# Exponential and normalising moved one step later in the chunk-band attention, and the stick-breaking gates loaded once, in a hybrid streaming encoder layer

## The chip, the core and the metric

The kernel runs on one core of one Trainium2 chip. The core has five engines that work side by side, each through its own list of instructions in the order of that list: PE (TensorE, matrix products and transposes), DVE (VectorE), ACT (ScalarE), POOL (GpSimd) and SP (SyncE, which here only issues transfers). The engines wait for each other by semaphores. The metric is the device time of one execution in microseconds (us); lower is better. Before the change it is 1001.7 us, the median of three runs from 1001.65 to 1001.97 us.

## What is computed

The reference is one layer of an encoder trunk over 1024 prompt tokens and 64 tokens of a running stream (whose past has 512 tokens). Everything is float32. Cut to what matters:

```python
h = rms_norm(x, norm_w) @ w_in                       # 1024 -> 6144 columns
sb_q, sb_k, sb_v, sb_z, cb_q, cb_k, cb_v, cb_z, g_sb, g_cb = split(h)
# branch A, "sb": stick-breaking attention, 8 heads x 64, causal over all keys
A[t, s] = beta[t, s] * prod_{s<j<t} (1 - beta[t, j]),   beta = sigmoid(q.k / 8)
# branch B, "cb": softmax attention over a band of 576 keys, with a bias by relative position
s = q.k / 8 + rel_bias[clip(q_pos - k_pos, -128, 128)]
p = softmax(s)
# merge
b_sb = (o_sb * silu(z_sb)) @ w_proj_sb
b_cb = (o_cb * silu(z_cb)) @ w_proj_cb
y = x + (sigmoid(g_sb) * b_sb + sigmoid(g_cb) * b_cb) @ w_out
```

A softmax of branch B is an exponential of the scores less their maximum, and a multiplication of each row by one over its sum. The keys, the values and `y` are outputs.

## The kernel before, in words

The kernel is written with an order of its own: every engine executes its instructions in the order in which the program emits them, and a tile framework adds the semaphores. A tile pool hands out a fixed number of buffers for each name; whoever takes a buffer again waits until the last reader of its earlier content is done.

**Stages.** The program first projects the input, then runs the attention of both branches, first all of "sb", then all of "cb", each as a list of steps (`seq`). It ends with the projection of "cb" and the output projection. A matrix product at full precision is split into three products of a high and a low part, so PE has much to do throughout.

**Attention steps.** One step is one head (or, for the stream tokens, both heads of a pair) with 128 query rows. Each branch has four pairs of heads, and each pair 17 steps: one for the stream tokens (`t == 8`, 576 keys) and two for each of eight blocks of 128 prompt tokens. In "cb" a block has 128 keys (t = 0) to 640 keys (t from 4 to 7), so 32 of its 68 steps have the full width of 640. The loop at the end of the attention code runs over steps `i`, and step `i` emits work for several of them:

- `qk(i)`: PE makes the scores `z` (two PSUM tiles when there are more than 512 keys, of three in the pool). For "cb" DVE adds the bias, negated, and keeps the row's minimum in `sm` (line 1041, two halves); then, as the last line of `qk`, ACT makes the exponential and its row sum (line 1045).
- `mid(i - 1)`: for "cb" DVE takes the reciprocal of the row sum (line 1058) and ACT multiplies the row by it (line 1059). `be` is the row of scores, exponentials and weights; it has four buffers.
- `tr(i - 3)` (`LAG` is 3): PE transposes the finished rows in blocks of 128 into PSUM tiles `pt` (line 1087; two buffers, up to four blocks in each), and ACT or DVE copies them to `wT` (lines 1096 and 1098). In "cb" every fourth of these copies is ACT's.
- `av`, one step after the second head of a pair of blocks: PE multiplies `wT` with the values into `o` (line 1126), and DVE multiplies that by the branch's gate z (line 1131).
- `fill`: between these parts PE gets matrix products that have nothing to do with the attention, by a count for each step.

**The filling work** comes from one generator, `run_fill`. It does eight units of 128 columns of the input projection (the gate columns of "cb", line 782, with a copy by ACT on line 757), and after these `proj_sb`, the projection of branch A. `proj_sb` is a list of twelve jobs `j`, four pieces of 256 output columns for three groups of tokens (384, 384 and 320, `CH`). Each job has two halves (`uu`): 12 matrix products into one of two PSUM tiles `acc` (line 882), and then a multiplication by the sigmoid of the branch's gate on DVE (line 886). That gate has been stored to DRAM before and comes back through `load_gate` (line 862): two transfers by SP into a tile `gt`, which has two buffers. Before the change a job loads the next job's gate at its start, and once more after the first half:

```python
            load(j + 1)                 # at the start of job j
            ...
                if uu == 0:
                    load(j + 1)         # again, after its first half
```

Where the second load takes the buffer that job j itself reads, SP cannot issue it before the multiplication of job j's second half, and SP's list stands until then.

**The end of the attention.** What remains of `proj_sb` after the last step (jobs 8 to 11 in part) runs by itself, and beside it the outputs of "cb" are read back from DRAM (line 839, `ot`, two buffers of two pairs each) and split into a high part on ACT (line 843) and a low part on POOL and DVE (line 848, `og`), for three groups of tokens. On DVE the two low parts of a group stand between the multiplications of `proj_sb`. The next group's outputs can be loaded only when the group before has been split. Then come the projection of "cb" (line 926) and the output projection (line 1429).

Of the kernel before, what the change touches and what calls it, by code (L numbers as in the profile page):

```python
# [32 lines left out]
def hybrid_step_kernel(ctx: ExitStack, tc: tile.TileContext, x_prompt, x_sample, c_sbk, c_sbv, c_cbk, c_cbv,  # L33
# [830 lines left out]
    def proj_sb(pool):  # L864
        load = lambda j: j < 12 and load_gate(pool, "gt", j, d_g["sb"][2 * (j // 3):2 * (j // 3) + 2], j % 3)
        for j in range(12):
            i, ci = divmod(j, 3)
            wh, wl = W.sp["p", i]
            a, e = CH[ci]
            load(j + 1)  # L870
            if ci == 0:
                load_proj(i + 2)
            if ci == 1:
                W.split(("p", i + 1))
            gt = gts.pop(j)
            for uu in range(2):
                cw = slice(uu * 128, uu * 128 + 128)
                ps = psF.tile([128, 512], F32, name="acc")
                for p in range(NPAIR):
                    gh, gl = og("sb", 0, p), og("sb", 1, p)  # L880
                    for m, (w, g) in enumerate(((wh, gh), (wh, gl), (wl, gh))):
                        TE.matmul(ps[:, :e - a], w[:, p, cw], g[:, a:e], start=p == 0 and m == 0,  # L882
                                  stop=p == NPAIR - 1 and m == 2)
                        if p < NPAIR - 1 or m < 2:
                            yield 1
                V.tensor_tensor(out=tb(2 * i + uu)[:, a:e], in0=ps[:, :e - a], in1=gt[:, uu, :e - a], op=OP.mult)
                if uu == 0:
                    load(j + 1)
                yield 1

    def load_gcb(j):
# [119 lines left out]
    def qk(i):  # L1011
# [17 lines left out]
        for j, (x, y) in enumerate(hs):  # L1029
# [10 lines left out]
            else:  # L1040
                V.tensor_tensor_reduce(be[:r, x:y], z[:r, :m], bt[:r, off + x:off + y], 1.0,  # L1041
                                       BIG if j == 0 else kp[:r, j - 1:j], OP.add, OP.min, kp[:r, j:j + 1])
        if b == "cb":
            j = len(hs) - 1
            A.activation(be[:r, :n], be[:r, :n], AF.Exp, bias=kp[:r, j:j + 1], scale=-1.0, accum_out=kp[:r, 2:3])  # L1045
        st[i] = (be, kp)

    def mid(i):
        b, p, t, hd = seq[i]
# [138 lines left out]
    for i in range(len(seq) + LAG + 1):  # L1188
        m = 0
        if i < len(seq):  # L1190
            b, p, t, hd = seq[i]
            if b == "cb" and p == 0 and t == 8 and hd == 0:
                sbx.close()
                yst = ExitStack()
                late["y"] = yst.enter_context(tc.tile_pool(name="ay", bufs=2))
            if (b, p, t, hd) == ("sb", 3, 6, 0):
                load_bias(0)
                load_bias(1)
            qk(i)
            if hd == 0:  # L1200
                if t % 2 == 1 or t == 8 and (b, p) != ("sb", 0):
                    load_z(b, p, t // 2 if t < 8 else 4)
                prefetch(b, p, t)
            acc += amount[b] * wt[b](band(b, t)[1]) / tot[b]
            if (b, p, t) == ("cb", 0, 8):
                acc += 12
            m = int(acc) - emitted
            emitted += m
        if 0 < i <= len(seq):
            mid(i - 1)  # L1210
        flush()
        if i < len(seq) and seq[i][:3] == ("cb", 0, 1) and hd == 1:
            late["sb"] = True
        fill(m // 2)
        while avq:
            av(*avq.pop(0))
        if 0 <= i - LAG < len(seq):
            tr(i - LAG)
            b, p, t, hd = seq[i - LAG]
            if t == 8 or hd == 1 and t % 2 == 1:  # L1220
                avq.append((b, p, t // 2 if t < 8 else 4))
        fill(m - m // 2)
# [292 lines left out]
```

## Time and profile before

The profiled execution took 1000.43 us, 1.27 us less than the median of the runs; its span is 998.6 us, and 1.8 us lie around the span.

| part | what it is | us |
|---|---|---|
| median of three runs | 1001.65 to 1001.97 | 1001.7 |
| profiled execution, whole | one run | 1000.43 |
| its span | first to last instruction | 998.6 |
| PE, matrix products | 97% of the span | 966.4 |
| DVE | 63% | 631.9 |
| ACT | 51% | 510.0 |
| POOL | 35% | 346.6 |

In the span the "cb" attention begins at about 673 us, its last products with the values end at 840 us, the last matrix product of `proj_sb` starts at 862 us, and the output projection starts at 911 us.

How to read the rows. A row of the timeline gives the start, the length, the engine, the line of the kernel, the operation and its tiles (out <- in, without buffer numbers), the shape and how many instructions are merged in it. The bracket at its end is the time that the engine was idle before it and what ended that wait. PEld is PE's loading of weights, which runs beside its products; SPq is the list of transfers that SP issues. A row of the windows gives, for a stretch of the span, each engine's busy time, then PE's granted clock (1.00 is full speed), the share of time that the 16 DMA engines were busy, and their rate in GB/s.

### The profile page before, as it was taken

The numbers are of one execution on the slowest core, as the hardware profiler recorded it, in microseconds if no ns is written. First come the engines' busy times: TensorE is split into PE (matmuls) and PEld (weight loads), VectorE is DVE, ScalarE is ACT, GpSimd is POOL, SyncE is SP. The second block draws the span as 40 slices with busy tenths as digits, with TensorE's granted clock in tenths as the row PEclk, the third lists the DMA queues.
The fourth block names the chain that finished last, engine by engine and source line by source line (L and its number), as shares of the span: only waits on it lengthen the run. The fifth ranks groups of instructions, "written<-read, shape, count | busy, mean of one in ns | idle before, by whom it ended". The sixth has DMA issues, their size and how long they took to land.

```text
span 998.6 us, 20448 instructions
## 1 busy us (share of the span) xinstructions
PE 966.4 (97%) x7568; PEld 917.9 (92%) x7568; DVE 631.9 (63%) x1188; ACT 510.0 (51%) x1142; POOL 346.6 (35%) x356
## 2 busy tenths in 40 slices
PE   5999999999999999999999999999899999899998
PEld 5999999999999999999988889888787877799998
DVE  5456674895455455432169899895676764589735
ACT  5544443444343433433268778786776774355320
POOL 3276663215445544542220110110201101286641
PEclk9999999999999999999999999999999999999999
DMA  6726577424656333332497567575788873853642
GB/s 229 232 95 219 190 249 257 149 91 149 199 156 189 104 94 110 121 108 73 138 254 203 151 164 197 145 212 162 225 241 244 245 208 97 260 170 99 196 137 89
DMA packets 177412, 171.04 MB, mean 171 GB/s; under 512 B 35040, under 2 KB 163168, under 8 KB 177184
## 3 DMA queue, kind: packets, MB, share of 16 engines
q1 hardware_dynamic: 168592, 161.41, 54.1%
q10 hardware_dynamic: 8720, 8.33, 2.6%
q8 instruction: 60, 0.98, 0.4%
q14 instruction: 40, 0.33, 0.1%
HBM read 110.96 MB, written 58.72 MB: 170 GB/s over the span
## 4 chain that ended last, share of the span: by engine, by line
PE 84%; ACT 5%; DVE 4%; DMA 3%; issue 2%; SPq 1%; POOL 1%; DVEq 0%; ACTq 0%
PE b L634 25%; PE acc L464 19%; PE b L1429 8%; PE o L1126 6%; PE acc L782 6%; PE pt L1087 5%; PE b L926 5%; PE z L1035 5%; PE acc L882 2%; DVE be L1041 1%; ACT be L1059 1%; ACT be L1045 1%; ACT wT L1096 1%; DMA wrawx<-in_w_in_dram 1%; PE pk L349 1%
## 5 line engine op out<-in xcount | busy, mean ns | idle before, releaser
L1087 PE MATMUL pt<-ident,be 128*128 128x128 f32 (+1 forms) x568 | 88.5, 278 | 10.0 <-ACT wT L1096 6.9
L122 POOL TENSOR_TENSOR wlo<-wraw,whi 128x1024 fp32r<-128x1024 f32 x22 | 57.2, 2598 | 107.9 <-ACT whi L115 107.7
L1055 DVE TENSOR_TENSOR_SCAN kp<-kp,imp 128x128 f32<-128x128 f32 (+7 forms) x64 | 88.3, 1379 | 0.6 <-ACT kp L1038 0.6
L1087 PEld LDWEIGHTS pt<-ident,be 128*128 128x128 f32 (+1 forms) x568 | 65.5, 140 | 23.0 <-ACT wT L1096 11.0
L1035 PE MATMUL z<-ks,sq 128*128 128x320 f32 (+5 forms) x384 | 83.5, 325 | 0.0
L464 PE MATMUL acc<-whi,xa 128*128 128x256 f32 x256 | 74.1, 292 | 0.0
L1096 ACT ACTIVATE wT<-pt 128x512 f32<-128x512 f32 (+3 forms) x125 | 58.3, 498 | 29.4 <-PE pt L1087 29.3
L464 PE MATMUL acc<-wlox,xm 128*128 128x256 f32 x256 | 70.7, 278 | 0.0
L464 PE MATMUL acc<-whi,xm 128*128 128x256 f32 x256 | 70.7, 278 | 0.0
L464 PE MATMUL acc<-wlo,xa 128*128 128x256 f32 x256 | 70.6, 278 | 0.0
L464 PE MATMUL acc<-whix,xb 128*128 128x256 f32 x256 | 70.6, 278 | 0.0
L464 PE MATMUL acc<-whix,xm 128*128 128x256 f32 x256 | 70.6, 278 | 0.0
L1126 PE MATMUL o<-wT,vp 128*64 128x256 f32 (+1 forms) x608 | 68.5, 357 | 2.0 <-ACT wT L1096 1.0
L1126 PEld LDWEIGHTS o<-wT,vp 128*64 128x64 f32 x608 | 42.7, 136 | 27.2 <-issue 5.9
L1035 PEld LDWEIGHTS z<-ks,sq 128*128 128x128 f32 x384 | 65.9, 188 | 1.3 <-DVE sm L1041 0.3
L1045 ACT ACTIVATE be<-be,sm 128x640 f32<-128x640 f32 (+5 forms) x68 | 47.4, 697 | 35.4 <-DVE sm L1041 34.8
L782 PE MATMUL acc<-xm,whi 128*128 128x384 f32 (+1 forms) x192 | 65.2, 340 | 0.0
L1056 DVE TENSOR_TENSOR be<-be,kp 128x128 f32<-128x128 f32 (+8 forms) x68 | 57.3, 843 | 9.4 <-ACT sg L757 0.5
L1038 ACT ACTIVATE kp<-z 128x384 f32<-128x384 f32 (+6 forms) x104 | 52.2, 502 | 10.1 <-PE z L1035 4.5
L642 DVE TENSOR_TENSOR u<-b,s 128x256 f32<-128x256 f32 (+1 forms) x48 | 20.8, 439 | 55.8 <-PE b L634 54.1
L1039 ACT ACTIVATE be<-z 128x384 f32<-128x384 f32 (+6 forms) x104 | 52.6, 506 | 0.0
L464 PEld LDWEIGHTS acc<-whi,xa 128*128 128x128 f32 x256 | 47.9, 188 | 0.1
(300 smaller groups left out, 3149.9 us busy)
## 6 DMA issues: line engine op xcount, KB each, us to landing
wraw<-in_w_in_dram SPq DMA_DIRECT2D x32, 512.0 KB, 4.5
wrawx<-in_w_in_dram SPq DMA_DIRECT2D x16, 512.0 KB, 4.3
sq<-d_qsbT SPq DMA_DIRECT2D x32, 192.0 KB, 3.6
sq<-d_qcbT SPq DMA_DIRECT2D x32, 192.0 KB, 4.2
gt<-d_gsb SPq DMA_DIRECT2D x30, 192.0 KB, 3.8
xt<-in_x_prompt_dram SPq DMA_DIRECT2D x8, 512.0 KB, 5.6
d_kcbT<-hl SPq DMA_DIRECT2D x8, 512.0 KB, 4.5
d_qcbT<-hl SPq DMA_DIRECT2D x8, 512.0 KB, 5.2
```

What stands on the lines that cost most here:

```text
L122: (eng or G).tensor_tensor(out=l, in0=raw, in1=h[:].bitcast(F32), op=OP.subtract)
L464: TE.matmul(ps, x, w, start=m == 0, stop=m == len(steps) - 1)
L634: TE.matmul(ps[:, :m], w[:, hl_, k], right[s](x)[:, k, a:b], start=s < 3 and k == 0 and e == 0, stop=k == 3 and e == 2, skip_group_check=s ...
L782: TE.matmul(ps[:, :b - a], w[:, k], xk(x, k)[:, a:b], start=k == 0 and n == 0, stop=k == KT - 1 and n == 2)
L1035: TE.matmul(z[:, :m], s[:, e, q0:q0 + 128], ks[:, h, o + x:o + y], start=e == parts[0][0], stop=e == parts[-1][0])
L1045: A.activation(be[:r, :n], be[:r, :n], AF.Exp, bias=kp[:r, j:j + 1], scale=-1.0, accum_out=kp[:r, 2:3])
L1055: V.tensor_tensor_scan(kp[:r, n - 1::-1], kp[:r, n - 1::-1], im[:, ::-1], 0.0, op0=OP.mult, op1=OP.add)
L1056: V.tensor_tensor(out=be[:r, :n], in0=be[:r, :n], in1=kp[:r, 1:n + 1], op=OP.mult)
L1087: TE.transpose(pt[:kr, x, :r], be[:r, kb * 128:kb * 128 + kr], ident[:r, :r])
L1096: A.activation(w[:, sl:sl + m, q0:q0 + r], pt[:, :m, :r], AF.Copy)
L1126: TE.matmul(o[hd * 64:hd * 64 + 64, c0:c1], vv[:kr, kb, hd * 64:hd * 64 + 64], wT[b, p, j, hd, s // 4][:kr, s % 4, c0:c1] if j < 4 else wT ...
L1429: TE.matmul(ps[:, t], left[s](xs_, k)[:, ts_], wt_[:, k], start=s < 3 and t == k == e == 0, stop=k == 3 and e == 2, skip_group_check=s > 2 ...
```

## The change

The exponential leaves `qk` and becomes `soft`, which step `i` calls for the "cb" step `i - 1`, ahead of its own scores. For "cb" `mid`, the reciprocal and the normalising, moves from step `i + 1` to step `i + 2`, also ahead of the scores. For "sb" `mid` stays where it was. The transposes of a row stay three steps behind its scores. And the second load of each gate in `proj_sb` goes.

```diff
@@ proj_sb
                 V.tensor_tensor(out=tb(2 * i + uu)[:, a:e], in0=ps[:, :e - a], in1=gt[:, uu, :e - a], op=OP.mult)
-                if uu == 0:
-                    load(j + 1)
                 yield 1
@@ qk, and the new soft
-        if b == "cb":
-            j = len(hs) - 1
-            A.activation(be[:r, :n], be[:r, :n], AF.Exp, bias=kp[:r, j:j + 1], scale=-1.0, accum_out=kp[:r, 2:3])
         st[i] = (be, kp)
+
+    def soft(i):
+        n = band(*seq[i][::2])[1]
+        be, kp = st[i]
+        j = 1 if n > 512 else 0
+        A.activation(be[:, :n], be[:, :n], AF.Exp, bias=kp[:, j:j + 1], scale=-1.0, accum_out=kp[:, 2:3])
@@ the loop over the steps
+        if 0 < i <= len(seq) and seq[i - 1][0] == "cb":
+            soft(i - 1)
+        if 1 < i <= len(seq) + 1 and seq[i - 2][0] == "cb":
+            mid(i - 2)
+        if i < len(seq):
             qk(i)
@@ the same loop, further down
-        if 0 < i <= len(seq):
+        if 0 < i <= len(seq) and seq[i - 1][0] == "sb":
             mid(i - 1)
```

Where this puts the instructions can be seen at three places. In the rows below, each `be` number is one step's row of scores, and `sm` with the next number is its small tile; the numbers differ between the two programs. Of four steps in a row, the first to the fourth, the rows are be_10514, be_10553, be_10592 and be_10627 before, and be_10502, be_10541, be_10580 and be_10615 after.

ACT, in the third pair of "cb" among steps of the full width, before: L1045 is the exponential, L1059 the normalising, L115 the split of a weight for `proj_sb`, L1096 a copy of transposed blocks (pt_10579 belongs to an earlier row, pt_10647 to be_10514).

```order
L115 ACTIVATE whi_10547<-wraw_9816 128x1024
L1045 ACTIVATE be_10553,sm_10554<-be_10553,sm_10554 128x640
L1059 ACTIVATE be_10514<-be_10514,sm_10515 128x640
L1096 ACTIVATE wT_10578<-pt_10579 128x4x128
L1045 ACTIVATE be_10592,sm_10593<-be_10592,sm_10593 128x640
L1059 ACTIVATE be_10553<-be_10553,sm_10554 128x640
L1045 ACTIVATE be_10627,sm_10628<-be_10627,sm_10628 128x640
L1059 ACTIVATE be_10592<-be_10592,sm_10593 128x640
L1096 ACTIVATE wT_10578<-pt_10647 128x3x128
```

The same place of ACT after the change, where L1047 is the exponential, L1060 the normalising and L1097 the copy; pt_10629 holds blocks of be_10502.

```order
L115 ACTIVATE whi_10532<-wraw_9813 128x1024
L1047 ACTIVATE be_10502,sm_10503<-be_10502,sm_10503 128x640
L1060 ACTIVATE be_10478<-be_10478,sm_10479 128x640
L1097 ACTIVATE wT_10563<-pt_10564 128x4x128
L1047 ACTIVATE be_10541,sm_10542<-be_10541,sm_10542 128x640
L1060 ACTIVATE be_10502<-be_10502,sm_10503 128x640
L1047 ACTIVATE be_10580,sm_10581<-be_10580,sm_10581 128x640
L1060 ACTIVATE be_10541<-be_10541,sm_10542 128x640
L1097 ACTIVATE wT_10563<-pt_10629 128x3x128
```

ACT's list keeps its kinds of work in the same order, but each exponential and each normalising in it is now that of the step before; the copies stay where they were.

DVE at the same place, before: L1041 is the addition of the bias with the row's minimum (two halves, each followed by a reading of the result), L1058 the reciprocal, L1098 a copy of transposed blocks, L1131 the product of an output with its gate.

```order
L1041 ISA be_10553,sm_10554<-z_10555,bias_9916 128x320
L1041 ISA sm_10554 128x1
L1041 ISA be_10553,sm_10554<-z_10559,bias_9916,sm_10554 128x320
L1041 ISA sm_10554 128x1
L1058 RECIPROCAL sm_10515<-sm_10515 128x1
L1131 TENSOR_TENSOR zt_10403<-o_10568,zt_10403 128x256
L1098 COPY wT_10585<-pt_10586 128x128
L1041 ISA be_10592,sm_10593<-z_10594,bias_9912 128x320
```

And DVE after the change (L1039 the addition of the bias, L1059 the reciprocal, L1132 the product, L1099 the copy).

```order
L1059 RECIPROCAL sm_10479<-sm_10479 128x1
L1039 ISA be_10541,sm_10542<-z_10543,bias_9912 128x320
L1039 ISA sm_10542 128x1
L1039 ISA be_10541,sm_10542<-z_10547,bias_9912,sm_10542 128x320
L1039 ISA sm_10542 128x1
L1132 TENSOR_TENSOR zt_10393<-o_10553,zt_10393 128x256
L1099 COPY wT_10570<-pt_10571 128x128
L1059 RECIPROCAL sm_10503<-sm_10503 128x1
L1039 ISA be_10580,sm_10581<-z_10582,bias_9908 128x320
```

The reciprocal of be_10514 (be_10502 after) has moved from behind its own step's successor to behind the product and the copy that follow, right ahead of the next scores.

SP, after the last step of the attention, before: the loads of the "cb" outputs (`ot`, groups of four), of the gates of `proj_sb` (`gt` from d_gsb6 and d_gsb7, two transfers each, for the jobs 9, 10 and 11) and of a weight.

```order
L862 DMA gt_11331<-d_gsb6_99 128x384
L862 DMA gt_11331<-d_gsb7_100 128x384
L862 DMA gt_11348<-d_gsb6_99 128x384
L862 DMA gt_11348<-d_gsb7_100 128x384
L862 DMA gt_11365<-d_gsb6_99 128x384
L862 DMA gt_11365<-d_gsb7_100 128x384
L826 DMA wraw_11368<-in_w_proj_cb_dram 128x4x128 x2
L862 DMA gt_11385<-d_gsb6_99 128x384
L862 DMA gt_11385<-d_gsb7_100 128x384
L839 DMA ot_11406<-d_ocb0_113 128x384
L839 DMA ot_11406<-d_ocb1_114 128x384
```

The same stretch of SP after the change.

```order
L862 DMA gt_11307<-d_gsb6_99 128x384
L862 DMA gt_11307<-d_gsb7_100 128x384
L862 DMA gt_11338<-d_gsb6_99 128x384
L862 DMA gt_11338<-d_gsb7_100 128x384
L826 DMA wraw_11341<-in_w_proj_cb_dram 128x4x128 x2
L839 DMA ot_11376<-d_ocb0_113 128x384
L839 DMA ot_11376<-d_ocb1_114 128x384
L839 DMA ot_11379<-d_ocb2_115 128x384
L839 DMA ot_11379<-d_ocb3_116 128x384
```

Between job 9's gate and the outputs of the second group, SP now has one load of job 10's gate where it had a second load of job 9's and two of job 10's. In the whole program 22 transfers of gates are gone, two for each of the jobs 1 to 11.

## The prediction

> **What bounds the kernel now.** I read the page's summary first, then the windows of the stretches that the change touches, then the list of waits in them, and last the timeline around the longest waits.
>
> ```profile
> span 998.6 us, 20448 instructions
> PE 966.4 (97%) x7568; PEld 917.9 (92%) x7568; DVE 631.9 (63%) x1188; ACT 510.0 (51%) x1142; POOL 346.6 (35%) x356
> ```
>
> PE is busy for 97% of the span, so a change that takes no work from PE can only win PE's idle time. How much of it lies where the change acts is read by stage:
>
> ```profile
> core 0: us, PE busy (x) PEld busy (x) DVE busy (x) ACT busy (x) POOL busy (x), PEclk, DMA share, GB/s
> 673.00:840.00 167.00, 157.26 (x1190) 133.34 (x1189) 111.10 (x396) 115.98 (x261) 16.98 (x22) 1.00 0.72 202
> 840.00:866.00 26.00, 21.12 (x117) 19.70 (x114) 9.24 (x14) 7.63 (x13) 6.74 (x6) 0.93 0.71 220
> 866.00:912.00 46.00, 46.00 (x285) 46.00 (x284) 41.39 (x54) 26.92 (x48) 32.01 (x26) 1.00 0.53 165
> ```
>
> In the "cb" attention (673 to 840) PE is idle for 167.00 - 157.26 = 9.74 us, while ACT and DVE are busy for only 69% and 67%: no engine is full, so the idle time comes from waiting in turn. In the stretch behind it, where `proj_sb` ends alone, PE is idle for another 4.88 us and its granted clock is below 1. In the 46 us after that PE never stops. The waits, with their total, their number and the longest, are these in the first of the stretches, and in the two together for the last three rows:
>
> ```profile
> PE pt L1087 <- ACT wT L1096: 6.3, 8, 1.7
> PE o L1126 <- ACT wT L1096: 1.0, 2, 0.5
> PE o L1126 <- DVE wT L1098: 0.8, 1, 0.8
> PE pt L1087 <- DVE wT L1098: 0.4, 1, 0.4
> ...
> PE acc L882 <- DVE xm L886: 4.9, 4, 3.5
> ACT be L1045 <- DVE sm L1041: 34.8, 34, 2.6
> DVE xm L886 <- DMA gt<-d_gsb: 8.4, 4, 3.6
> ```
>
> Twelve waits of 8.5 us in all hold PE in the attention, ten of them on a copy by ACT. PE wants a PSUM tile for the next transposes, and the copy out of it stands in ACT's list behind an exponential, which waits 34 times for the scores of the newest step. In the last stretch PE waits 4.9 us for DVE's multiplication by the gate, which waits for the gate's transfer.
>
> **Part 1, the exponential and the normalising.** Nothing is added: the same 68 exponentials, reciprocals and normalising copies, and one table load. What moves is where ACT stands when it has to wait. One of the twelve waits shows it:
>
> ```profile
> 785.51 0.83 ACT L1045 ACTIVATE be<-be,sm 128x640 f32<-128x640 f32 x1 [0.95 <-DVE sm L1041]
> 786.34 0.82 ACT L1059 ACTIVATE be<-be,sm 128x640 f32<-128x640 f32 x1
> 786.74 0.71 PE L1087 MATMUL pt<-ident,be 128*128 128x128 f32 x5
> 787.53 0.83 ACT L1045 ACTIVATE be<-be,sm 128x640 f32<-128x640 f32 x1 [0.37 <-DVE sm L1041]
> ...
> 789.08 0.47 ACT L1096 ACTIVATE wT<-pt 128x384 f32<-128x384 f32 x1
> ...
> 789.60 0.77 PE L1087 MATMUL pt<-ident,be 128*128 128x128 f32 x5 [0.68 <-ACT wT L1096]
> ```
>
> PE's transposes are done at 787.45, but ACT copies them only at 789.08: it waited for DVE until 787.53, then made an exponential and a normalising. With the change the pair ahead of that copy is the one of the step before, which ran here from 785.51 to 787.16, so ACT stands ready when the transposes are done. The copy comes some 1.6 us sooner, and the 0.68 us are won. I did the same for each of the twelve; three keep something.
>
> ```profile
> 680.13 1.14 PE L1087 MATMUL pt<-ident,be 128*128 128x128 f32 x8 [1.28 <-ACT wT L1096]
> ...
> 835.85 0.77 PE L1087 MATMUL pt<-ident,be 128*128 128x128 f32 x5 [0.53 <-ACT wT L1096]
> ```
>
> The wait at 835.85 and the one of 0.4 us on DVE's copy, which follows it, belong to the last steps, where PE has no filling work; they stay, since there ACT needs a reciprocal that DVE makes behind copies of fresh transposes, before the change and after it. The wait at 680.13, at the start of "cb", keeps about half, some 0.6 us, because ACT's table load then falls into the next step. That leaves 8.5 - 0.9 - 0.6 = 7.0 us of waits to win.
>
> What is late next: a row's normalising comes a step later and its transposes do not, so only about half a step lies between them, where it was a step and a half. Where ACT has extra work, that is used up:
>
> ```profile
> 699.98 1.05 ACT L115 ACTIVATE whi<-wraw 128x1024 fp32r<-128x1024 f32 x1
> 701.34 0.82 ACT L1045 ACTIVATE be<-be,sm 128x640 f32<-128x640 f32 x1
> 702.15 0.82 ACT L1059 ACTIVATE be<-be,sm 128x640 f32<-128x640 f32 x1
> ...
> 702.34 0.77 PE L1087 MATMUL pt<-ident,be 128*128 128x128 f32 x5
> ...
> 706.66 0.83 ACT L1045 ACTIVATE be<-be,sm 128x640 f32<-128x640 f32 x1 [1.74 <-DVE sm L1041]
> ...
> 709.25 0.44 PE L1087 MATMUL pt<-ident,be 128*128 128x128 f32 x2 [1.69 <-ACT wT L1096]
> ```
>
> Here a weight's split fills ACT from 699.98. With the change the normalising at 702.15 is that of the very row that PE transposes at 702.34, so PE would wait until 702.97, a new 0.6 us; the 1.69 us at 709.25 go, as ACT's 1.74 us of waiting at 706.66 go. I count four such new waits of 0.55 us, for the splits and the reading of "sb" outputs that share ACT with full steps: 2.2 us. On DVE the reciprocal now stands ahead of the newest scores. It needs an exponential that ACT makes first in the step before; I cost it at nothing, covered by most of that step; the cover fails only where ACT is over a step late, and then each us of that holds up the scores, and PE, a PSUM tile further on, by as much. SP, POOL and PE keep their order in this part, and no transfer moves with it. The sum of part 1 is 7.0 - 2.2 = 4.8 us. The trace of before does not show the short spare time itself; its ends are 7.5 us won (no new wait, and all but the two last old ones gone) and a loss, priced below. I take a value nearer to the upper end, because the row at 787.53 is the common case and the one at 702.15 has a split, a gate copy and an output's high part in one step.
>
> **Part 2, the gates.** 22 transfers go, 14 of 192 KB and 8 of 160 KB, 4.0 MB. In the attention they share a queue that is busy for 72%, and PE waits for no transfer there; that share of them I cost at nothing, hidden under the attention steps, and what it costs if the cover fails is the wait on a gate: DVE waited 8.4 us for gates in four places. The gain is in the end of `proj_sb`:
>
> ```profile
> 843.44 5.02 SPq L862 DMA_DIRECT2D gt<-d_gsb  x6
> ...
> 848.66 0.56 DVE L886 TENSOR_TENSOR xm<-acc,gt 128x384 f32<-128x384 f32 x1 [3.63 <-DMA gt<-d_gsb]
> ...
> 851.31 0.54 DVE L886 TENSOR_TENSOR xm<-acc,gt 128x384 f32<-128x384 f32 x1
> 851.88 0.81 SPq L862 DMA_DIRECT2D gt<-d_gsb  x2
> ...
> 852.79 1.80 SPq L839 DMA_DIRECT2D ot<-d_ocb  x4
> ...
> 857.65 2.21 DVE L848 TENSOR_TENSOR og<-ot,og 128x384 fp32r<-128x384 f32 x2 [2.83 <-ACT og L843]
> 859.78 0.54 DVE L886 TENSOR_TENSOR xm<-acc,gt 128x384 f32<-128x384 f32 x1
> ...
> 856.58 0.31 PE L882 MATMUL acc<-xa,wlo 128*128 128x320 f32 x1
> 860.38 0.41 PE L882 MATMUL acc<-xa,whi 128*128 128x320 f32 x1 [3.49 <-DVE xm L886]
> ```
>
> Read backwards: PE stands at 860.38 for the multiplication of 859.78; that stands on DVE behind the low parts of 857.65; these wait for outputs that SP issued at 852.79, behind the second load of a gate at 851.88, which had to wait for the multiplication of 851.31. The multiplication of 848.66 waits for a gate whose first load was issued at 843.44 and whose second one counts. Without the second loads that gate is there one landing after 843.9, and with
>
> ```profile
> gt<-d_gsb SPq DMA_DIRECT2D x30, 192.0 KB, 3.8
> ```
>
> that is 847.7. The multiplication ends at 848.2, the two low parts of the first group, which stand behind it on DVE as those of the second do at 857.65 and take as long (2.2 us), at 850.4, and then SP, with nothing held ahead, issues the last two of the four outputs; before, those two came at 852.79 + 0.9 = 853.7. So the rest of the chain comes 3.3 us earlier, and PE goes on at 857.1 instead of 860.38. It will have come to that place at about 854.9: before, it was there at 856.58 + 0.31, and some 2 us of that were shorter pauses for the two multiplications ahead. So it still stands for some 2.2 us. The ends for this term are 1.5 us (the outputs land no sooner than half of this gain) and 4.9 us (no pause at all). Then there is the clock behind the pause:
>
> ```profile
> 862.00:863.00 1.00, 1.00 (x6) 1.00 (x5) 0.14 (x1) 0.00 (x0) 0.00 (x0) 0.50 0.90 310
> ...
> 700.00:720.00 20.00, 17.63 (x130) 1.00 0.81 240
> 861.00:866.00 5.00, 5.00 (x23) 0.66 0.83 258
> ```
>
> (The first row has all engines, the other two PE alone.) After the pause of 3.49 us the granted clock fell to 0.50 and was 0.66 on the mean of 5 us: 5 x 0.34 = 1.7 us lost. After the pause of 1.69 us at 709.25 the window kept 1.00. A pause of 2.2 us lies between the two; the shorter one is nearer (0.5 against 1.3 us), so I take the 1.7 us as won, with 0 and 1.7 as ends. The Trainium skill says in "TensorE: Matmul & The Clock Gate", part 1, that the clock halves after at least one idle window of about 3.4 us that runs freely; by that rule a pause of 2.2 us cannot halve it, and both pauses above agree with it.
>
> The stage behind, 866 to 912, could take the gain back, since DVE is 90% busy there; but PE waited for nothing in it, DVE's work starts from the same transfers and moves with it, and I take nothing off. Part 2 is 3.3 + 1.7 = 5.0 us.
>
> **Sum.** 4.8 + 5.0 = 9.8 us. Against the profiled execution that is 1000.43 - 9.8 = 990.6 us; that run was 1.3 us below the median of three, and against the median it is 1001.7 - 9.8 = 991.9 us.
>
> **Rivals.**
> - *Only the gates tell.* For each old wait on ACT's copy a new one on the normalising comes, as at 702.34. For it: ACT works without a break in the rows from 699.98 to 702.97. Against it: 34.8 us of ACT's waiting go. Part 1 is 0: 1001.7 - 5.0 = 996.7 us.
> - *The last pause stays.* The outputs land late for another reason (queue 71% busy), PE stands for 3.49 us again and the clock halves again. For it: in the row of 857.65 DVE waits for ACT, not for a gate. Against it: SP's order in the rows of 851.88 and 852.79. 1001.7 - 4.8 = 996.9 us.
> - *Slower: the normalising becomes the wait of every full step.* PE's transposes come where ACT has just begun the row. The price at 702.34 is 0.6 us; in all 32 full-width steps it is 19.2 us, and the time 1001.7 + 19.2 - 9.8 = 1011.1 us. It decides from 9.8 / 32 = 0.3 us a step. Against it: ACT is 69% busy, so it cannot be late in each step.
> - *No change*: PE's work is the same, and the waits come back elsewhere, on DVE's copies for instance; within 0.2% of 1001.7.
>
> **How the numbers follow.** 0.2%, 2.0 us, is about what a measurement of this kernel can tell from no change. Both parts, 988 to 996 us: 0.60. Only the gates, 996.7: 0.12. The last pause stays, 996.9: 0.08. Below 988: 0.05; the floor is 1001.7 - 9.74 - 4.88 - 1.7 = 985.4. Within 0.2%: 0.06. The slower rival: 0.09. So faster is 0.60 + 0.12 + 0.08 + 0.05 = 0.85. The range goes from the upper ends, 7.5 + 4.9 + 1.7 = 14.1 below (987.6, given as 988), to 999, where part 1 gives about 1 and part 2 its lower 1.5; it holds the first three cases, 0.80.
>
> **What would show it.** Right: in the "cb" attention PE's idle time falls from 9.7 to about 5 us, and ACT's waits for DVE's scores almost vanish; some PE waits name the normalising. SP shows 16 gate loads of 192 KB for 30, the outputs are issued some 3 us sooner after the attention's end, and PE's clock stays at 1.00. Wrong: PE waits at many transposes for ACT's normalising, or DVE's reciprocals wait for the exponential and hold up the scores; or the pause at the last job is still over 3 us.

## The result, and the profile after

The changed kernel takes 986.89 us, the median of four runs from 986.66 to 988.42 us; the kernel before took 1001.84 us in the same comparison. The ratio is 0.984, with a 95% interval from 0.980 to 0.988. The forecast was 991.9 us, with a range from 988 to 999: the direction was right, but the time lies below the range, where the forecast had put a chance of 0.05. The gain of 14.9 us is half as large again as the 9.8 us forecast.

The page's summary of the changed kernel:

```profile
span 985.0 us, 20439 instructions
PE 962.0 (98%) x7568; PEld 917.6 (93%) x7568; DVE 630.1 (64%) x1188; ACT 510.4 (52%) x1142; POOL 346.2 (35%) x356
```

Its profiled execution has a span 13.6 us shorter than the one before. Where they went is read from windows cut at the same points of the program: the copy of the last gate columns ahead of "cb", the start of the last product with the values, the first product of the projection of "cb", the first of the output projection. Before:

```profile
core 0: us, PE busy (x) PEld busy (x) DVE busy (x) ACT busy (x) POOL busy (x), PEclk, DMA share, GB/s
672.97:840.30 167.33, 157.59 (x1193) 133.64 (x1192) 111.13 (x396) 116.01 (x261) 16.98 (x22) 1.00 0.71 202
840.30:862.60 22.30, 17.43 (x100) 16.02 (x99) 8.75 (x13) 5.00 (x9) 6.67 (x5) 0.98 0.70 217
862.60:910.90 48.30, 48.30 (x288) 48.30 (x288) 40.81 (x54) 28.63 (x50) 30.98 (x25) 0.97 0.56 175
```

And after:

```profile
673.75:831.80 158.05, 154.21 (x1193) 133.67 (x1192) 109.34 (x396) 116.82 (x261) 17.00 (x22) 1.00 0.70 195
831.80:849.30 17.50, 16.19 (x101) 15.75 (x100) 7.58 (x13) 4.99 (x9) 7.08 (x5) 1.00 0.68 207
849.30:896.40 47.10, 47.10 (x289) 47.10 (x288) 40.72 (x53) 27.96 (x48) 30.74 (x24) 1.00 0.58 182
```

The attention is 167.33 - 158.05 = 9.3 us shorter, the tail of `proj_sb` 4.8 us, and the projection of "cb" 1.2 us, since it no longer begins at the halved clock. Against that "cb" begins 0.8 us later, and some 0.9 us are given back in the output projection (the last section): 9.3 + 4.8 + 1.2 - 0.8 - 0.9 = 13.6.

The first row of each group holds the surprise. The same 1193 products are in both; PE's idle time falls by 9.74 - 3.84 = 5.9 us, and its busy time falls as well, by 3.4 us. The weight loads are busy for the same 133.6 us, so their idle time must fall by the whole gain of 9.3 us; what tells more is that the waits named in their rows fall from 17.2 to 8.2 us. These are the waits that are left in the attention, PE's, ACT's (up to 852 us) and two of the weight loads':

```profile
PE pt L1088 <- ACT be L1060: 1.4, 2, 0.9
PE pt L1088 <- ACT wT L1097: 0.9, 2, 0.5
PE pt L1088 <- DVE wT L1099: 0.8, 2, 0.5
ACT be L1060 <- DVE sm L1059: 9.2, 15, 2.3
ACT be L1047 <- DVE sm L1039: 3.4, 10, 0.5
PEld pt L1088 <- ACT be L1060: 2.8, 4, 1.1
PEld pt L1088 <- ACT wT L1097: 2.0, 5, 0.7
```

Six waits of 3.1 us hold PE where twelve of 8.5 us did. ACT's 34.8 us of waiting for the scores have become 3.4, with 9.2 us for the reciprocals beside them. PE's two waits for the normalising (L1060) are new:

```profile
712.61 0.90 SPq L839 DMA_DIRECT2D ot<-d_osb  x2
...
715.75 0.52 ACT L843 ACTIVATE xa<-ot 128x384 fp32r<-128x384 f32 x1 [2.28 <-DMA ot<-d_osb]
...
716.99 0.81 ACT L1060 ACTIVATE be<-be,sm 128x640 f32<-128x640 f32 x1
...
717.86 0.92 PE L1088 MATMUL pt<-ident,be 128*128 128x128 f32 x5 [0.88 <-ACT be L1060]
```

The forecast looked for such waits at the splits of weights and at the reading of "sb" outputs. They came with the second alone, and by its lateness: ACT waited 2.28 us for an output of "sb" from DRAM, and exponential and normalising stood behind it. In the tail:

```profile
839.14 1.02 DVE L848 TENSOR_TENSOR og<-ot,og 128x384 fp32r<-128x384 f32 x2
...
839.75 1.76 SPq L839 DMA_DIRECT2D ot<-d_ocb  x4
...
844.66 2.25 DVE L848 TENSOR_TENSOR og<-ot,og 128x384 fp32r<-128x384 f32 x2 [1.80 <-ACT og L843]
...
847.43 0.42 PE L882 MATMUL acc<-xa,whi 128*128 128x320 f32 x1 [1.31 <-DVE xm L886]
```

The second group of outputs is issued 8.0 us behind the attention's last products instead of 12.5, PE's last pause is 1.31 us instead of 3.49, and the clock stays at 1.00 (third row of the windows).

### The profile page after: what moved, and what is told of

Its sections match the earlier page's. It is cut to its first block, busy times and chain, and to the rows that moved or that the text cites. A ratio compares the mean times of both kernels' runs of the same rounds, so it can differ in the third digit from the quotient of the medians.

```text
span 985.0 us, 20439 instructions
## 1 busy us (share of the span) xinstructions
PE 962.0 (98%) x7568; PEld 917.6 (93%) x7568; DVE 630.1 (64%) x1188; ACT 510.4 (52%) x1142; POOL 346.2 (35%) x356
## 4 chain that ended last, share of the span: by engine, by line
PE 90%; DMA 3%; ACT 3%; DVE 1%; SPq 1%; issue 1%; POOL 1%; DVEq 0%; ACTq 0%
PE b L634 25%; PE acc L464 19%; PE b L1435 8%; PE o L1127 7%; PE acc L782 7%; PE z L1033 6%; PE pt L1088 6%; PE b L924 5%; PE acc L882 3%; DMA wrawx<-in_w_in_dram 1%; PE pk L349 1%; ACT wT L1097 1%; PE pt L277 1%; SPq L51 1%; PE acc L1471 1%
## 5 line engine op out<-in xcount | busy, mean ns | idle before, releaser
L1097 ACT ACTIVATE wT<-pt 128x512 f32<-128x512 f32 (+3 forms) x125 | 58.6, 501 | 39.0 <-PE pt L1088 38.9
L1060 ACT ACTIVATE be<-be,sm 128x640 f32<-128x640 f32 (+5 forms) x68 | 47.2, 694 | 9.5 <-DVE sm L1059 9.2
L1047 ACT ACTIVATE be<-be,sm 128x640 f32<-128x640 f32 (+5 forms) x68 | 47.2, 694 | 3.7 <-DVE sm L1039 3.4
```

The lines of the kernel that those rows point to most:

```text
L1097: A.activation(w[:, sl:sl + m, q0:q0 + r], pt[:, :m, :r], AF.Copy)
```

## The experiments

The question is where the 5 us beyond the forecast came from. Theory A held that both parts did what was said and add up, and that a pause of PE is dearer than its idle time. The rivals put the rest down to the transfers that went, to one of the two moves alone, or to the waits of the second loads. Each run was compared with the kernel before, whose median in these comparisons was 1001.5 to 1003.0 us; so a difference of 1 to 2 us between two runs of different comparisons is not sure.

**Each part alone.** From the kernel before, only the second load is removed:

```diff
-                if uu == 0:
-                    load(j + 1)
```

> Only the second loads of the gates are removed; exponential and normalising stand as before. Theory A (the two parts add up, and the attention's gain of 9.3 us belongs to the re-timing): in the attention PE's 9.7 us of idle time stay, the stretch from the last product with the values to the projection of cb is about 4.8 us shorter, the granted clock stays at 1.00 after the last pause; time 1001.8 - 6 = 995.8 us. Rival B (the transfers that go also free the attention: part of its 9.3 us is theirs): the attention is 2 to 4 us shorter here too, time about 992 us.

Measured: 996.42 us (994.99 to 997.94; ratio 0.994, interval 0.993 to 0.996), a gain of 5.1 us. The attention takes 167.5 us in its profile, as before (though at a clock of 0.99, to which the last section comes back), and the tail is 4.1 us shorter:

```profile
673.01:840.50 167.49, 158.55 (x1194) 135.47 (x1192) 111.44 (x396) 116.04 (x261) 16.97 (x22) 0.99 0.68 185
```

Theory A's reading of the gates alone holds, and rival B's 992 us does not come. The other half is the changed kernel with the second load put back:

```diff
+                if uu == 0:
+                    load(j + 1)
```

> Only the exponential and the normalising are moved; each gate is still loaded twice. Theory A: the attention is 9.3 us shorter, the tail keeps its pause of 3.5 us and the clock of 0.50 behind it; time 1001.8 - 9.3 = 992.5 us. Rival B: the attention is only 5 to 7 us shorter, time 995 to 997 us.

Measured: 1001.71 us (998.42 to 1003.94; ratio 0.9995, interval 0.998 to 1.001). Both theories miss. Alone, the re-timing wins nothing. So the parts do not add up: 5.1 + 0 apart, 14.9 together. The profiled execution is the longest of the twelve (1003.94 us), and its attention of 169.9 us is 2.6 us longer than before:

```profile
672.76:842.70 169.94, 157.82 (x1194) 136.91 (x1192) 109.74 (x396) 117.02 (x261) 17.27 (x22) 0.98 0.73 199
```

It shows what took the gain (three pieces of its timeline):

```profile
757.93 0.41 PE L1035 MATMUL z<-ks,sq 128*128 128x128 f32 x2 [1.34 <-DMA sq<-d_qcbT]
...
785.25 0.42 DVE L1134 TENSOR_TENSOR zt<-o,zt 128x256 f32<-128x256 f32 x1 [3.45 <-DMA zt<-d_zcb]
...
792.59 0.56 DVE L886 TENSOR_TENSOR xm<-acc,gt 128x384 f32<-128x384 f32 x1 [3.58 <-DMA gt<-d_gsb]
793.07 0.42 DVE L1101 COPY wT<-pt 128x256 f32<-128x256 f32 x1
...
793.53 0.69 PE L1090 MATMUL pt<-ident,be 128*128 128x128 f32 x2 [3.22 <-DVE wT L1101]
```

Queries, the gate z and the gate of `proj_sb` all land late. DVE stands for a gate with the copy of transposes behind it, and PE stands for the copy. Where ACT's copies no longer hold PE, the transfers do. The mean clock of 0.98 is up to 3.4 us of it: twice the clock fell to 0.50, behind the pause of 3.22 us and one of 2.28 us at 718.25.

**Which move counts.** In the changed kernel (gates loaded once) the normalising goes back behind the scores, and only the exponential stays moved:

```diff
-        if 1 < i <= len(seq) + 1 and seq[i - 2][0] == "cb":
-            mid(i - 2)
...
-        if 0 < i <= len(seq) and seq[i - 1][0] == "sb":
+        if 0 < i <= len(seq):
             mid(i - 1)
```

> As the changed kernel (gates loaded once), but only the exponential is moved; the normalising of a row follows in the same step, behind the scores, as before. Theory A (what costs is that ACT waits for fresh work of DVE ahead of a copy): ACT's wait moves from the exponential to the normalising, whose reciprocal stands on DVE behind the newest scores, so the copies stay late; little of the 9.3 us is won, 993 to 996 us. Rival C (the exponential is the long step and its place alone decides): 987 to 989 us, as the changed kernel.

Measured: 996.21 us (995.08 to 996.65), 0.2 us from the gates alone and as much above theory A's 993 to 996. Rival C falls. ACT's waiting moved to the normalising, as theory A had it:

```profile
ACT be L1060 <- DVE sm L1059: 31.6, 68, 3.5
DVE sm L1059 <- ACT be L1047: 21.8, 32, 2.1
```

With 34.8 us of it at the exponential before, that is nearly the same sum. The reverse, where only the normalising is moved and the exponential is made at the end of `qk` again:

```diff
+        if b == "cb":
+            soft(i)                      # at the end of qk(i)
...
-        if 0 < i <= len(seq) and seq[i - 1][0] == "cb":
-            soft(i - 1)
```

> As the changed kernel (gates loaded once), but only the normalising is moved; the exponential is made at the end of its own step's scores, as before. Theory A: the exponential still makes ACT wait for DVE's scores ahead of the copy; what is won is only the 0.8 us of the normalising between the two, on some of the twelve waits: 991 to 995 us. Rival C: none of the 9.3 us is won, 996 us, since the exponential's place decides alone.

Measured: 987.86 us (987.58 to 989.51; ratio 0.986, interval 0.984 to 0.988): 8.6 of the 9.5 us between 996.4 and 986.9. Both theories miss: A had the mechanism, but gave it 1 to 5 us. ACT still waits 10.9 us at the exponential and 12.6 us at the normalising there. I read it so: what counts is that a row's normalising is out of the way before ACT has to wait for the next scores. The move takes DVE's reciprocal along with ACT's multiplication, and which of the two does it was not tested apart.

**What the second loads cost in the re-timed attention.** First they come back only during the attention (8 of 11), then only behind it (3):

```diff
+                if uu == 0 and att_open[0]:          # the other run: not att_open[0]
+                    load(j + 1)
```

> The changed kernel, in which the same 8 second loads come back during the attention, into the gate's own tile, as before; behind the attention each gate is loaded once. It has SP's list and the transfers of the kernel with the spare tile, and the waits in addition. Theory D: 995 to 998 us, with DVE waiting some 3.5 us for a gate in one or two places of the attention and PE for DVE's copies behind it. Rival E: the same time as the kernel with the spare tile, within 1 us.

> The changed kernel with the second loads back only behind the attention (3 loads, 6 transfers). If the shares add up, the cost of these (here x), of those in the attention (993.2 - 986.9 = 6.3 us) and the changed kernel make up the kernel with all second loads (1001.7 us): x = 8.5 us, 995.4 us. If only the tail of the kernel before counts (the 5.1 us of the gates alone), it is 992.0 us. The pause at the last job is 3.5 us again, with the clock at 0.50 behind it.

Measured: 993.19 us (991.62 to 995.35) and 993.42 us (991.90 to 996.46), so 6.3 and 6.5 us above the changed kernel. The first is below theory D's 995 to 998, and 1.7 us below the kernel with the spare tile (next run), where rival E had 1 us at most; the second lies between its two values. Together they give 999.7 us, 2.0 us short of the kernel that has all of them. In the tail the pause is back at 3.44 us, and the granted clock is 0.50 from 854 to 856 us. The tail takes 23.7 us there for 17.5; the attention, which has no second loads, is 1.6 us longer, with the clock halved behind a pause of 1.72 us at 718.67.

Then the second loads of the attention go into a tile that nobody reads: the same list and bytes, no wait for a buffer and no wait by DVE.

```diff
+                if uu == 0 and j < 11 and att_open[0]:
+                    spare(j + 1)                     # the same two transfers, into gx
```

> The changed kernel, in which the second load of a gate comes back during the attention (8 loads, 16 transfers, about 3 MB), at the same place of SP's list and with the same data, but into a tile of its own that nobody reads. So the traffic is there and the waiting is not. Theory D (in the attention the second loads cost by waiting: SP's list stands for the multiplication that frees the buffer, and DVE's next multiplication waits for the later of two loads): 987 to 989 us, as the changed kernel. Rival E (they cost by the traffic of a queue that is busy for 70%): 994 to 999 us.

Measured: 994.93 us (994.01 to 995.15; ratio 0.992). Theory D falls: with no wait of its own the traffic costs 8.0 us, no less than the 6.3 us of the same loads with their waits. It makes other transfers late. DVE's waits for the gate z, after the change and in this kernel:

```profile
DVE zt L1132 <- DMA zt<-d_zcb: 1.9, 1, 1.9
```

```profile
DVE zt L1142 <- DMA zt<-d_zcb: 8.8, 4, 3.1
```

What of it is bytes, and what is places in SP's list? An eighth of the bytes, at the same places:

```diff
-            SP.dma_start(gx[:, w, :e - a], d[:, a:e])
+            SP.dma_start(gx[:, w, :48], d[:, a:a + 48])
```

> As the kernel with the spare tile (994.9 us), but each of the 16 second transfers brings 48 columns instead of 384 or 320, an eighth of the bytes; their number and their places in SP's list are the same. Theory E1 (the second loads cost by their bytes: other transfers land late in a queue that is busy for 70 to 75%): 987 to 989 us, near the changed kernel. Rival E2 (they cost by their places: 0.45 us of SP for each issue, and the waits of SP's list around them): 993 to 995 us, as with full loads.

All the bytes, but issued by POOL:

```diff
-            SP.dma_start(gx[:, w, :e - a], d[:, a:e])
+            G.dma_start(gx[:, w, :e - a], d[:, a:e])
```

> As the kernel with the spare tile (994.9 us): the same 16 second transfers with all their bytes at the same point of the program, but issued by POOL instead of SP. Theory E1 (bytes): 992 to 996 us. Rival E2 (places in SP's list): 987 to 990 us. With the run of an eighth of the bytes (989.7 us) the estimate is 994.9 - 2.8 = 992 us, if the two shares simply add up.

Measured: 989.67 us (988.17 to 993.38) with few bytes and 994.24 us (992.57 to 995.16) by POOL. The first is 0.7 us above theory E1's range, the second lies in it, and rival E2 falls in both. The bytes are most of it: without them 5.3 of the 8.0 us go, without the places in SP's list 0.7, which is within the noise. The shares don't add up exactly; the first run spreads over 5 us. The clock is not what parts them: the executions with a mean clock of 0.999 to 1.000 took 995.15 us with all bytes by SP, 995.16 by POOL, and 989.67 with few. The Trainium skill says in "DMA: Bandwidth & Descriptors", section "Rules for kernel authors", that spreading transfers over several issuing engines does not raise the bandwidth, because all use the same 16 engines; the run with POOL agrees.

**A later transpose.** The new waits for the normalising suggested more time between it and the transposes: in "cb" the transposes come four steps behind the scores. (A first form changed the "sb" attention too.)

```diff
-        if 0 <= i - LAG < len(seq):              # LAG = 3
-            tr(i - LAG)
+        k = next((i - n for c, n in (("sb", LAG), ("cb", 4))      # first form: LAG = 4
+                  if 0 <= i - n < len(seq) and seq[i - n][0] == c), None)
+        if k is not None:
+            tr(k)
...
-        be = am.tile([128, NP], F32, name="be", bufs=4)
+        be = am.tile([128, NP], F32, name="be", bufs=5)
```

> The changed kernel with the transposes four steps behind the scores instead of three, and five buffers of be for four. Theory A (the waits of 0.88 and 0.52 us for the normalising at 717.86 and 719.82 come from the short time that the change left between normalising and transposes): these two go, which is worth 1.4 + 2 x 0.3 = 2.0 us, but the attention ends with one more step without filling work, some 1 us: 985 to 987 us. Rival G (the spare time isn't short anywhere; the waits come from an overloaded ACT and only move): 987 to 989 us.

> The changed kernel with the transposes four steps behind the scores in the cb attention alone (three in sb, as before), and five buffers of be for four; it parts the question from the earlier run, in which the sb attention changed too. Theory A (short time between normalising and transposes): the waits of 0.88 and 0.52 us at 717.86 and 719.82 go, the end of the attention gets one more step without filling work: 985 to 987 us. Rival G (that time is short only where ACT is held by a late transfer; elsewhere a later transpose brings nothing, and the additional step at the end costs 1 to 2 us): 987.5 to 989.5 us.

Measured: 992.87 us (991.02 to 994.06) and 992.19 us (990.34 to 993.81); all theories miss. The two waits are gone, and others came:

```profile
774.48 1.30 SPq L109 DMA_DIRECT2D wraw<-in_w_proj_sb_dram  x1
778.58 0.32 SPq L1105 DMA_DIRECT2D zt<-d_zcb  x1
...
787.30 2.47 SPq L51 DMA_DIRECT2D sqs<-d_qcbT  x4
```

```profile
790.69 0.50 PE L1033 MATMUL z<-kss,sqs 128*128 128x288 f32 x2 [2.15 <-DMA sqs<-d_qcbT]
```

SP stands from 775.78 to 778.58 ahead of `zt`; in the changed kernel it issues the same transfer without a stop. A `zt` buffer is freed by a step's output, which now comes a step later, so the queries further down SP's list land late and PE waits 2.15 us. That the buffer is what SP waits for is read from the order, not tested. This pause and the clock of 0.50 behind it are the largest piece of the 5.3 us that were lost; the rest was not traced.

**The pauses that are left.** The count that places the second split behind the attention is raised:

```diff
-        fill((46, 24, 100000)[ci])
+        fill((46, 36, 100000)[ci])
```

> The changed kernel with one count altered: behind the attention the second group of the cb outputs is split after 36 matrix products instead of 24, so that on DVE the multiplication for which PE waited 1.31 us at 847.43 stands ahead of the two low parts. Theory A (that pause is set by DVE's order, and a pause costs its idle time and 0.3 us more): 986.9 - 1.6 = 985.3 us, no pause behind the attention. Rival F (the last outputs are then late, and the projection of cb or DVE in it takes the gain back): 986.5 to 988 us.

Measured: 985.15 us (984.61 to 986.02; ratio 0.983, interval 0.981 to 0.984), 1.7 us better than the changed kernel, as theory A had it; the two intervals overlap, so the amount is not sure, but the tail is: it takes 15.9 us for 17.5, without a pause; the attention still has the wait for the late output, in this profile of 1.86 us and with the clock at 0.50 behind it. Loading the "sb" outputs further ahead, on top of that:

```diff
-                ots[ci, p] = stage.tile([128, 384], F32, name="ot", bufs=4)
+                ots[ci, p] = stage.tile([128, 384], F32, name="ot", bufs=6)
+                            load_og("sb", 1, late["y"], [0, 1])   # and each later piece two earlier
```

> The kernel with the later split behind the attention (985.15 us), in which the sb outputs that proj_sb needs are loaded further ahead: six buffers of ot for four, five pieces ahead for three. Theory J (at 716 ACT waits 2.3 us for such an output, and so the normalising is late at 717.86 and 719.82, with a chance that the clock halves behind it): the two waits of 1.4 us and their ends go, 983 to 984 us, and the granted clock stays at 1.00 around 718 us. Rival G2 (the pauses come from ACT's work there, not from the transfer): 985 us, with the same two waits.

Measured: 985.42 us (982.65 to 987.95). Theory J is right at its place (0.17 us is left of the two waits, and the clock is 1.00 around 718 us), but the time is the same within a spread of 5 us: waits of 0.91 us for DVE's scores and 0.60 us for queries came elsewhere. And the gates of the jobs 1 to 8 loaded by POOL, on top of the later split:

```diff
-            SP.dma_start(gts[key][:, w, :e - a], d[:, a:e])
+            (eng or SP).dma_start(gts[key][:, w, :e - a], d[:, a:e])     # eng = G for j < 9
```

> The kernel with the later split behind the attention (985.15 us), in which the gates of the jobs 1 to 8 are loaded by POOL, which is busy for 17 of 158 us in the attention, instead of SP. Theory K (SP's list, which issues for 100 of 110 us from 690 to 800, still holds the attention back): the 16 issues of some 0.5 us leave the list, 982 to 984 us. Rival L (the list has enough slack once the second loads are gone): 985 to 986 us.

Measured: 985.41 us (984.64 to 988.42); rival L holds.

**The price of a pause.** PE gets one PSUM tile for transposed blocks instead of two:

```diff
-    psT = att.enter_context(tc.tile_pool(name="at", bufs=2, space=PS))
+    psT = att.enter_context(tc.tile_pool(name="at", bufs=1, space=PS))
```

> The changed kernel with one PSUM tile for the transposed blocks instead of two, so that PE waits at nearly every group of transposes in both attentions. Theory H (a pause costs its idle time and 0.25 to 0.45 us more, which the page counts as busy): the time grows by PE's additional idle time plus 0.25 to 0.45 us for each additional wait of PE. Rival I (PE's idle time tells the price of pauses): the time grows by PE's additional idle time alone, and PE's busy time stays at 962 us.

Measured: 1066.66 us (1061.47 to 1068.14). The page's summary and PE's two largest waits:

```profile
span 1066.3 us, 20424 instructions
PE 984.8 (92%) x7568; PEld 920.8 (86%) x7568; DVE 635.4 (60%) x1188; ACT 517.5 (49%) x1142; POOL 342.9 (32%) x356
```

```profile
PE pt L1088 <- ACT wT L1097: 43.0, 52, 2.6
PE pt L1088 <- DVE wT L1099: 21.2, 28, 0.9
```

The span grows by 81.3 us. PE's idle time grows by (1066.3 - 984.8) - (985.0 - 962.0) = 58.5 us, and the other 22.8 us are counted as busy. The idle time of the weight loads grows by (1066.3 - 920.8) - (985.0 - 917.6) = 78.1 us, nearly the whole, since they are busy for about as long as before. Rival I falls, and theory H holds in kind. Its amount can't be parted from the clock, whose mean fell to 0.987: 22.8 us over some 74 additional waits are at most 0.31 us each, and if all of the (1 - 0.987) x 1066.3 = 13.9 us that the clock withheld are in them, 0.12 us (an estimate). Theory H's upper 0.45 us is not reached.

## Why the prediction was right in sign and wrong in size

Two steps failed: in part 1 the price of a wait, and in part 2 the transfers of the attention, put at nothing, with the sum that took the two parts as independent. The attention gave 9.3 us for 4.8 forecast; what lies behind it gave 6.0 for 5.0.

- *What bounds the kernel, and the sign:* right. PE's pauses were what could be won, and the floor of 985.4 us, from PE's idle time, was nearly reached, with 3.8 + 1.3 us of that idle time still there. So it isn't a floor: busy time can fall too.
- *The old and new waits of part 1 (7.0 won, 2.2 new):* nearly right as idle time. 8.5 us became 3.1, so 5.4 us were won where 4.8 were forecast. The waits at 835.85 and after it stayed, as said, and the one at 680.13 kept 0.47 us for 0.6. The new ones are two of 1.4 us, not four of 2.2, and at another place, behind a late transfer.
- *The price of each wait (failed):* the sum took PE's idle time for what a wait costs. The last product ahead of a pause is seen as busy until it has run out, where in a stream the next one lies over it (products of 0.34 us start 0.17 us apart). The wait of 0.81 us at 743.40 was worth 1.12 us: PE's lead in the changed kernel grows from 2.55 us at the product of 741.95 to 3.67 at that of 745.03. The one of 0.67 us at 752.28 was worth 0.89, and a wait of 0.58 us at 811.26 is seen on the weight loads alone. So I read the 3.4 us by which PE's busy time fell in the attention (the clock is 1.00 in both windows); the rows of the weight loads before the change would have told it:

```profile
PEld pt L1087 <- ACT wT L1096: 8.6, 9, 1.9
PEld o L1126 <- ACT wT L1096: 3.1, 5, 1.0
```

 These two alone hold 11.7 us, where PE's rows for the same waits hold 7.3; after the change they hold 2.9.
- *The pair of exponential and normalising:* it was costed as one. The normalising is worth 8.6 us by itself and the exponential 0.2 (with the gates loaded once).
- *Transfers in the attention "at nothing", and the sum of two parts (failed):* nearly right for the kernel before (167.5 us of attention without the second loads, 167.3 with them; 1.7 of the 167.5 are a halved clock, which the other profile hasn't, so as much may be hidden), wrong for the sum. Alone, part 2 gave its 5.0 us (5.1) and part 1 nothing of its 4.8: that part 1 won at all hung on part 2. With the re-timing done, the second loads in the attention cost 6.3 us. Part 1 was costed on "PE waits for no transfer there", which was true only while ACT's copies held PE. The DMA share of 72% was a mean over the stretch; inside it the queue is fuller, in the kernel before and after it:

```profile
690.00:800.00 110.00, 103.89 (x773) 88.60 (x771) 75.86 (x280) 80.38 (x180) 14.58 (x21) 1.00 0.86 241
```

```profile
690.00:800.00 110.00, 108.01 (x838) 94.17 (x837) 77.75 (x291) 84.62 (x192) 14.60 (x21) 1.00 0.85 236
```

 In the same 110 us, with the queue as full, PE now does 838 products instead of 773. Each part alone left the other limit standing. That the queue is the second limit is shown by the runs with spare bytes; that 236 to 241 GB/s is its end is not shown.
- *The tail (3.3 + 1.7):* right in its chain, and a little low. The outputs came 4.5 us sooner instead of 3.3: the two low parts of the first group ahead of them took 1.02 us (839.14) where 2.2 were put. Why they are quicker there stays open. The pause is 1.31 us instead of 2.2, and the tail with the projection behind it won 6.0 us.
- *The rivals:* "only the gates tell" is what the gates alone do (996.4 us for 996.7). It was no rival to the full change, but the value of one of its halves. The slower one has no support: no step waits for the normalising but at the late output.

## What to carry to other kernels

Price PE's waits by those that are named in the rows of its weight loads rather than by PE's own, and count every pause, also the short ones. Before adding up the parts of a change, ask of each what would hold the engine next if the others were in place; read a queue's share in the stretch where it is fullest, not over the stage. And a transfer that costs nothing today can cost its full share once the wait that covers it is gone.

## What the runs showed of the hardware that was not expected

A pause of PE does not decide the clock by its length alone. The same pause, after the same work, in the kernel before (its row of the timeline, then PE's busy time, clock and DMA load in a window right behind it):

```profile
709.25 0.44 PE L1087 MATMUL pt<-ident,be 128*128 128x128 f32 x2 [1.69 <-ACT wT L1096]
```

```profile
710.00:711.00 1.00, 1.00 (x9) 1.00 0.36 103
```

And in the kernel with only the gates changed:

```profile
709.27 0.44 PE L1085 MATMUL pt<-ident,be 128*128 128x128 f32 x2 [1.70 <-ACT wT L1094]
```

```profile
710.00:711.00 1.00, 1.00 (x5) 0.50 0.30 85
```

One execution kept 1.00, the other ran at 0.50 for 3.4 us and lost 1.7 us. In the re-timed kernel a pause of 2.28 us at 718.25 was followed by 0.50 from 719 to 721, while in the one with the gates alone a pause of 2.02 us at 856.81 was not. The Trainium skill ("TensorE: Matmul & The Clock Gate", part 1) calls the window free-running, which fits the same pause going both ways; its length of about 3.4 us as the least idle time does not fit, and here the measurement decides.

Where the pause lies matters too. In the profiled executions of all kernels here but the one with a single PSUM tile, no pause under 1.69 us was followed by 0.50 (the start and the end of the program aside), and all five from 3.2 us on were. Of the 17 between, from 1.69 to 2.28 us, 10 of the 11 in the attentions were followed by it, and none of the 6 behind the attention, the longest of these 2.02 us. Each time 0.50 lasted 3.4 or 6.8 us, so 1.7 or 3.4 us were lost. Why the place matters stays open. The forecast's 2.2 us behind the attention that "cannot halve it" was thus not refuted there, but it was no safe reading for a pause in the attention. Over 17 runs of the kernel before, the mean granted clock was 0.994 to 0.998, in the four of the changed kernel 0.998 to 1.000.

In the output projection the changed kernel waits 0.21 us for a weight at 920.42, and from then until 939 its products start 0.118 us apart, where they start 0.113 us apart in the kernel before; the granted clock reads 1.00 all the while. PE's lead over the kernel before falls from 14.5 to 13.5 us on the way. That is the 0.9 us given back, and its cause stays open.
